# Pinning GpSimd's and TensorE's order in a loop over 64 experts, and taking GpSimd's weight splits to VectorE

## The chip, the cores and the metric

The kernel runs on one core of one Trainium2 chip. The metric is device time in microseconds of one execution. In the profile PE is TensorE, DVE is VectorE, ACT is ScalarE, POOL is GpSimd and SP is SyncE, which here only issues DMAs.

## What is computed

One layer of a hybrid decoder for 520 tokens (512 of a prompt, 8 samples), d_model 1024: a state-space branch and a dilated-attention branch, a layer norm, then a mixture of 64 experts (each token goes to 8), a shared expert, a gated per-layer input and a second layer norm. The change lies in the mixture of experts alone:

```python
scores = jax.nn.sigmoid(jnp.einsum('nd,de->ne', xf, w['w_router']))
_, top_idx = lax.top_k(scores + w['router_bias'], TOP_K)
...
    xb = x_pad[tok]
    h = jax.nn.silu(xb @ w1[e]) * (xb @ w3[e])
    yb = (h @ w2[e]).astype(jnp.float32)
    return acc.at[tok].add(yb * g[:, None])
...
shared = (jax.nn.silu(xf @ w['ws1']) * (xf @ w['ws3'])) @ w['ws2']
```

## The kernel before, in words

Every f32 product is made of three fp32r products: a matrix is split into `hi` (its value rounded by ACT) and `lo` (the rest, a subtraction on another engine), and hi x hi, lo x hi and hi x lo are summed in PSUM (`split`, line 267).

The weights of an expert are six chunks of 128x1024 floats: four (`AT`) for the first product, 1024 to 512 columns, and two (`BT`) for the second, 256 to 1024. The class `Stream` (line 288) loads them through SP into 12 raw buffers (`raw2` and `pre`), and splits them into five pairs of buffers (tag `v`, `VB`). Chunks are listed in the order in which PE takes them: four of expert e, two of expert e-1. Line 333 gives the subtraction of one chunk in six to POOL, 63 in all; the rest are DVE's.

The experts are sorted by the number of their tokens, and `CAPS` holds the rows that each place may take, from 112 down to 56. The loop is at line 1599; round e has these pieces:

- `expert_in(e)` (line 1429): 24 matmuls of 512 columns with four chunks, then `ffn_mid`: a SiLU on ACT and a product on DVE (`hg`).
- `turn(e + 1)` (line 1418): eight transposes of the gathered rows `xg` of the next expert, and their split (`xgh` on ACT, `xgl` on DVE).
- `expert_out(e - 1)` (line 1437): 12 matmuls with two chunks, `y` (scaled by the gates) on ACT, and a scatter with addition by POOL into `accD` in DRAM (line 1451). There are two such sums; experts below `SECOND` = 50 alternate between them, later ones use the first.
- `ffn_turn(e)` (line 1258): the turning of the inner layer, two transposes of `hg` and their split (`hh`, `hl`).
- `fetch(e + 3)` (line 1408): `find` searches the rows of an expert by five small matmuls with a one-hot matrix (`oh`, of DVE) into the PSUM tile `x`, which DVE reduces (`both`) and makes into row numbers (`idx`); `gather` (line 1412) has POOL fetch those rows from DRAM into one of three buffers `xg`.
- From round 6 on a piece of side work in four of five rounds (lines 1621 to 1632): parts of the shared expert (`shared_more`, `shared_out`), the per-layer inputs (`layer_inputs`, 30 matmuls of 256 columns, 20 times), and at the end `second_sums` (line 1372), which loads the second DRAM sum through SP into a single buffer and adds it to the residual on POOL.

The side work and the search share the only buffer of the PSUM pool `psx` (line 1481). The tile framework puts every engine's instructions into an order by a planner that simulates the program. What `tc.keep_in_program_order` marks keeps the order of the program on its engine. For PE the flag `T.pinned` (line 207) does so; it is off in the loop.

Of the kernel before, what the change touches and what calls it, by code (L numbers as in the profile page):

```python
# [11 lines left out]
def _quiet(*args, **kwargs):  # L12
# [11 lines left out]
ALU = mybir.AluOpType  # L24
# [4 lines left out]
NT = 520  # L29
HALF = 260  # L30
TT = 104
NE = 64
FIXED = 2
CAPS = ([112] * 3 + [100] * 1 + [94] * 1 + [92] * 1 + [88] * 2 + [86] * 1 + [84] * 3 + [82] * 2 + [78] * 7 + [76] * 2 + [74] * 4
        + [72] * 5 + [70] * 4 + [68] * 4 + [66] * 5 + [64] * 7 + [62] * 3 + [60] * 2 + [58] * 2 + [56] * 5)
# [16 lines left out]
SECOND = 50  # L52
# [148 lines left out]
def trunk_step(ctx: ExitStack, tc: tile.TileContext, I, O):  # L201
    nc = tc.nc
    V, S, G = nc.vector, nc.scalar, nc.gpsimd
# [15 lines left out]
    T = Tensor()  # L219
# [41 lines left out]
    def add(e, o, a, b):  # L261
        return e.tensor_tensor(out=o, in0=a, in1=b, op=ALU.add)
# [4 lines left out]
    def split(hi, lo, src, e=V):  # L267

        a = S.activation(hi, src, AF.Copy)  # L269
        return a, sub(e, lo, src, hi.bitcast(F32))  # L270
# [17 lines left out]
    class Stream:  # L288
# [34 lines left out]
        def split_to(self, n):  # L323
            while self.done < min(n, len(self.srcs)):
                p, tag, bufs = self.pools(self.done, 1)
                if p is None:
                    return
                self.load_to(self.done + 1)
                raw, was = self.raw.pop(self.done)
                hi = p.tile([128, 1024], F32R, tag=tag + "h", bufs=bufs, name="hi")  # L330
                lo = p.tile([128, 1024], F32R, tag=tag + "l", bufs=bufs, name="lo")
                m = self.done - P2 - 2
                split(hi, lo, raw, G if 0 < m < 6 * (NE - 1) and m % 6 == 2 else V)
                self.parts[self.done] = (hi, lo)
                self.done += 1
                self.held[was] -= 1
                self.load_to(self.done + 40)
# [7 lines left out]
    P2 = 48  # L345
    AT, BT = {}, {}

    H, EX = {}, {}
# [67 lines left out]
    xD = dram.tile([NT, 1024], F32, name="xD")  # L416
    sumsD = [dram.tile([640, 1024], F32, name=f"accD{n}") for n in range(2)]
# [840 lines left out]
    def ffn_turn(hg, m):  # L1258
        ps = bank()
        for k in range(2):  # L1260
            T.transpose(ps[:, m * k:m * k + m], hg[0:m, 128 * k:128 * k + 128], ident[0:m, 0:m])
        hh, hl = (moe.tile([128, 2, MAX_CAP], F32R, tag=nm, bufs=2, name=nm)[:, :, 0:m] for nm in ("hh", "hl"))
        H['turned'] = split(hh, hl, ps[:, 0:2 * m].rearrange("p (k t) -> p k t", k=2))
        return hh, hl
# [94 lines left out]
    def last_scales(i):  # L1359

        if i < 0:
            H['ln2'] = pw.tile([TT, 2, 1024], F32, tag="ph", name="ln2")
            H['rows'] = pw.tile([1, 2, 1024], F32, tag="pl", name="rows")
            nc.sync.dma_start(H['rows'], I['rows'][None, 2:4])
        else:
            for h in range(2):
                c = slice(512 * h, 512 * h + 512)
                ps = psx.tile([128, 512], F32, tag="x", name="x")[0:TT]
                T.matmul(ps, lhsT=H['ones'], rhs=H['rows'][:, i, c], start=True, stop=True)
                S.activation(H['ln2'][:, i, c], ps, AF.Copy)  # L1370

    def second_sums(i):

        t = pw.tile([128, 1024], F32, tag="praw", name="second")[0:TT]
        nc.sync.dma_start(t, sumsD[1][TT * i:TT * i + TT])
        add(G, H['x1'][:, i], H['x1'][:, i], t)


    XG, XT, HG, HT, GC, IX = {}, {}, {}, {}, {}, {}

    OH = {}

    def find(e, what=(0, 1)):

        m = CAPS[e]
        if e not in OH:
            OH[e] = one_hot(e, m)
# [19 lines left out]

    def fetch(e):
        find(e)
        gather(e)  # L1410

    def gather(e):
        m = CAPS[e]
        G.indirect_dma_start(out=XG[e % 3][0:m], out_offset=None, in_=xD[:, :],  # L1414
                             in_offset=bass.IndirectOffsetOnAxis(ap=IX[e][0:m, 0:1], axis=0),
                             bounds_check=NT - 1, oob_is_err=False)

    def turn(e):
        x, m = XG[e % 3], CAPS[e]
# [17 lines left out]
    def expert_out(e):  # L1437
        ps, m = mm2(), CAPS[e]
        hh, hl = HT.pop(e)
        for k in range(2):  # L1440
            hi, lo = stream.get(BT[e] + k)
            for n, (l, w) in enumerate(((hh, hi), (hh, lo), (hl, hi))):
                for h in range(2):
                    T.matmul(ps[0:m, h], lhsT=l[:, k], rhs=w[:, 512 * h:512 * h + 512], start=(k == 0 and n == 0),
                             stop=(k == 1 and n == 2))
        if e >= NE - 2:
            kept(e, ps)
            return
        y = py.tile([MAX_CAP, 1024], F32, tag="y", bufs=YB, name="y")[0:m]
        S.activation(y.rearrange("p (h n) -> p h n", h=2), ps[0:m], AF.Copy, scale=GC.pop(e)[0:m])  # L1450
        G.indirect_dma_start(out=sumsD[e % 2 if e < SECOND else 0][:, :], out_offset=bass.IndirectOffsetOnAxis(ap=IX.pop(e)[0:m, 0:1], axis=0),  # L1451
                             in_=y, in_offset=None, compute_op=ALU.add)

    def kept(e, ps):

# [21 lines left out]
    def second_phase():  # L1477
# [9 lines left out]
        x1 = H['x1']  # L1487
# [108 lines left out]
        py = open_pool("py")  # L1596
        side = [(q, i) for q in range(-2, 4) for i in range(-1, 5)]
        side += [(4, -1), (4, 0), (4, 1)] + [(5, i) for i in R5]
        for e in range(NE + 1):
            if e == NE - 1:  # L1600
                last_rows()
            if 0 < e < NE:
                expert_in(e)
            if 0 < e < NE - 1:
                turn(e + 1)
            if e:
                expert_out(e - 1)
            else:
                H['shared'] = py.tile([128, 5, 2, 2, TT], F32R, tag="side", name="st")
                mids = py.tile([MAX_CAP, 1024], F32, tag="y", bufs=YB, name="mids")  # L1610
                mids = [shared_mid(H['first half'][i], mids[0:TT, 128 * i:128 * i + 128]) for i in R5]
            if 0 < e < 6:
                shared_turn(mids[e - 1], e - 1, 0)
            if 0 < e < NE - 1:
                HT[e] = ffn_turn(HG.pop(e), CAPS[e])
            if e + 3 < NE:
                fetch(e + 3)
            if e == 4:
                close_pool(pre)
                pw = open_pool("pw")  # L1620
            while side and (e - 4) * SIDE >= N_SIDE - len(side) + 1:
                q, i = side.pop(0)
                if q == -2:
                    shared_more(i)
                elif q == -1:
                    shared_out(i)
                elif q < 4:
                    layer_inputs(q, i)
                elif q == 5:
                    second_sums(i)  # L1630
                else:
                    last_scales(i)
        assert not side
        acc = {}
        for i in R5:
# [216 lines left out]
```

## Time and profile before

| what | us |
|---|---|
| median of 3 runs | 1363.4 |
| lowest and highest of them | 1359.24, 1363.55 |
| the profiled execution | 1371.03 |
| its span, from the first to the last instruction | 1369.2 |
| busy in the span: PE, DVE, ACT, POOL | 1191.9, 970.3, 700.3, 560.2 |
| PE's mean granted clock | 0.928 of full |

The profile is of one execution; a busy time is the time in which an engine had an instruction under way, and the busy times of engines overlap. A matmul's row is longer than the distance to the next one, since matmuls are pipelined, so that PE's pace is read from the starts. A wait names what ended last before an instruction started. The granted clock is 1 at 2.4 GHz and 0.5 at 1.2 GHz. The DMA share is the mean busy share of the 16 DMA engines.

### The profile page before, as it was taken

What the parts mean: (1) busy time and instruction counts of PE and PEld (TensorE: products, weight loads), DVE (VectorE), ACT (ScalarE), POOL (GpSimd) and SP (SyncE); (2) the same over time, 40 slices, a digit from 0 to 9 for tenths busy, and PEclk for the clock granted to TensorE, in tenths of its full rate; (3) what the DMA queues carried; (4) which work ended last, traced back from release to release, by engine and by line L of the source; (5) the groups of instructions that cost most, each with busy time, mean ns of one, the idle gap of its engine ahead of it and who ended that gap; (6) DMA issues with size and microseconds to landing.
All of it is one profiled execution on the core that took longest, in us unless ns stands there. A gap on an engine that the chain in (4) does not pass through costs nothing. (4 is left out here: it accounts for less than half of the span.)

```text
span 1369.2 us, 20382 instructions
## 1 busy us (share of the span) xinstructions
PE 1191.9 (87%) x7082; PEld 890.2 (65%) x7084; DVE 970.3 (71%) x1397; ACT 700.3 (51%) x1055; POOL 560.2 (41%) x327
## 2 busy tenths in 40 slices
PE   7699899999997979787899688899999998968783
PEld 7699799999877756565566466576666664434441
DVE  7873748633588877576788578789789777647656
ACT  4131534222213766566567456767567665546562
POOL 1821231010124436243565354465664644464326
PEclk9898899999997989898999899999999999788896
DMA  7476553442512989798899798999999899887773
GB/s 286 134 240 120 191 182 105 118 116 92 191 60 89 294 222 314 226 286 262 257 319 319 224 274 275 310 306 305 303 300 321 288 301 266 224 229 243 260 191 100
DMA packets 114182, 312.93 MB, mean 229 GB/s; under 512 B 36986, under 2 KB 37410, under 8 KB 113000
## 3 DMA queue, kind: packets, MB, share of 16 engines
q1 hardware_dynamic: 68892, 249.24, 54.2%
q0 software_dynamic: 30208, 41.20, 14.0%
q10 hardware_dynamic: 14974, 21.14, 5.9%
q8 instruction: 57, 0.93, 0.3%
q14 instruction: 51, 0.42, 0.1%
HBM read 276.32 MB, written 32.87 MB: 226 GB/s over the span
## 5 line engine op out<-in xcount | busy, mean ns | idle before, releaser
L265 DVE TENSOR_TENSOR lo<-raw,hi 128x1024 fp32r<-128x1024 f32 x371 | 552.6, 1503 | 170.1 <-ACT hi L269 166.0
L269 ACT ACTIVATE hi<-raw 128x1024 fp32r<-128x1024 f32 x434 | 450.9, 1056 | 253.4 <-DMA raw<-in_we_dram 80.0
L1451 POOL DMA_INDIRECT accD<-y,idx x62 | 137.0, 2210 | 267.2 <-ACT hh L269 118.2
L210 PE MATMUL a<-hi,xgh 128*64 128x512 f32 (+18 forms) x512 | 211.8, 414 | 8.8 <-DVE xgl L265 6.0
L210 PE MATMUL a<-lo,xgh 128*64 128x512 f32 (+18 forms) x512 | 210.1, 410 | 7.3 <-DVE lo L265 7.3
L210 PE MATMUL a<-hi,xgl 128*64 128x512 f32 (+18 forms) x512 | 206.9, 404 | 0.0
L265 POOL TENSOR_TENSOR lo<-raw,hi 128x1024 fp32r<-128x1024 f32 x63 | 169.3, 2687 | 46.6 <-ACT hi L269 34.8
L1414 POOL DMA_INDIRECT xg<-xD,idx x64 | 125.0, 1953 | 146.5 <-DVE idx L1396 105.1
L210 PE MATMUL mm<-xh,hi 128*128 128x260 f32 (+1 forms) x576 | 121.7, 293 | 19.1 <-DVE r L259 10.7
L210 PE MATMUL mm<-xl,hi 128*128 128x260 f32 (+1 forms) x576 | 120.2, 291 | 0.8 <-DVE xl L265 0.8
L210 PE MATMUL mm<-xh,lo 128*128 128x260 f32 (+1 forms) x576 | 120.5, 291 | 0.0
L210 PEld LDWEIGHTS a<-hi,xgh 128*64 128x64 f32 (+18 forms) x512 | 75.7, 148 | 53.3 <-DVE xgl L265 7.6
L210 PEld LDWEIGHTS a<-lo,xgh 128*64 128x64 f32 (+18 forms) x512 | 75.6, 148 | 48.4 <-DVE lo L265 11.6
L210 PEld LDWEIGHTS mm<-xh,hi 128*128 128x128 f32 x576 | 92.8, 197 | 20.1 <-issue 11.0
L210 PE MATMUL mm<-lo,hh 128*64 128x512 f32 (+18 forms) x256 | 88.3, 428 | 18.3 <-POOL lo L265 17.8
L210 PEld LDWEIGHTS a<-hi,xgl 128*64 128x64 f32 (+18 forms) x512 | 75.5, 147 | 41.1 <-issue 4.0
L215 PE MATMUL a<-ident,xg 64*128 64x64 f32 (+18 forms) x512 | 57.7, 243 | 46.8 <-DMA xg<-xD,idx 38.5
L215 PEld LDWEIGHTS a<-ident,xg 64*128 64x128 f32 (+18 forms) x512 | 49.6, 148 | 73.0 <-DMA xg<-xD,idx 26.4
L210 PE MATMUL mm<-hi,hh 128*64 128x512 f32 (+18 forms) x256 | 88.0, 425 | 8.8 <-ACT hh L269 8.8
L1450 ACT ACTIVATE y<-mm,both 78x1024 f32<-78x1024 f32 (+19 forms) x62 | 68.8, 1109 | 52.1 <-PE mm L210 35.4
L210 PEld LDWEIGHTS mm<-xl,hi 128*128 128x128 f32 x576 | 92.2, 195 | 1.3 <-DVE xl L265 1.1
L210 PEld LDWEIGHTS mm<-xh,lo 128*128 128x128 f32 x576 | 92.4, 195 | 0.1
(410 smaller groups left out, 1999.1 us busy)
## 6 DMA issues: line engine op xcount, KB each, us to landing
raw<-in_we_dram SPq DMA_DIRECT2D x384, 512.0 KB
raw<-in_wd_dram SPq DMA_DIRECT2D x50, 512.0 KB
accD<-zeros_b POOLq DMA_DIRECT2D x2, 2560.0 KB
praw<-in_wp_dram SPq DMA_DIRECT2D x8, 512.0 KB
base<-in_xtok_dram ACTq DMA_DIRECT2D x1, 2080.0 KB
xD<-base ACTq DMA_DIRECT2D x5, 416.0 KB
second<-accD SPq DMA_DIRECT2D x5, 416.0 KB
acc<-accD SPq DMA_DIRECT2D x5, 416.0 KB
```

The lines of the kernel that those rows point to most:

```text
L210: ins = nc.tensor.matmul(*a, **k)
L215: ins = nc.tensor.transpose(*a, **k)
L265: return e.tensor_tensor(out=o, in0=a, in1=b, op=ALU.subtract)
L269: a = S.activation(hi, src, AF.Copy)
L1414: G.indirect_dma_start(out=XG[e % 3][0:m], out_offset=None, in_=xD[:, :], in_offset=bass.IndirectOffsetOnAxis(ap=IX[e][0:m, 0:1], axis=0), ...
L1450: S.activation(y.rearrange("p (h n) -> p h n", h=2), ps[0:m], AF.Copy, scale=GC.pop(e)[0:m])
L1451: G.indirect_dma_start(out=sumsD[e % 2 if e < SECOND else 0][:, :], out_offset=bass.IndirectOffsetOnAxis(ap=IX.pop(e)[0:m, 0:1], axis=0), ...
```

## The change

`split` of weight chunks is always ACT's and DVE's. `second_sums` adds on DVE. The expert's scatter is cut out of `expert_out` into a function of its own, `scatter`; gathers and scatters are kept in program order, which is now the gather of e+4, then the scatter of e-1 (round 0 fetches 3 and 4). `T.pinned` is on in the loop, and in PE's program order `ffn_turn(e)` stands at the end of the round, behind the side work.

```diff
--- before.py
+++ after.py
@@ -329,8 +329,7 @@
                 raw, was = self.raw.pop(self.done)
                 hi = p.tile([128, 1024], F32R, tag=tag + "h", bufs=bufs, name="hi")
                 lo = p.tile([128, 1024], F32R, tag=tag + "l", bufs=bufs, name="lo")
-                m = self.done - P2 - 2
-                split(hi, lo, raw, G if 0 < m < 6 * (NE - 1) and m % 6 == 2 else V)
+                split(hi, lo, raw)
                 self.parts[self.done] = (hi, lo)
                 self.done += 1
                 self.held[was] -= 1
@@ -1373,12 +1372,12 @@
 
         t = pw.tile([128, 1024], F32, tag="praw", name="second")[0:TT]
         nc.sync.dma_start(t, sumsD[1][TT * i:TT * i + TT])
-        add(G, H['x1'][:, i], H['x1'][:, i], t)
+        add(V, H['x1'][:, i], H['x1'][:, i], t)
 
 
     XG, XT, HG, HT, GC, IX = {}, {}, {}, {}, {}, {}
 
-    OH = {}
+    OH, YE = {}, {}
 
     def find(e, what=(0, 1)):
 
@@ -1407,13 +1406,13 @@
 
     def fetch(e):
         find(e)
-        gather(e)
+        tc.keep_in_program_order(gather(e))
 
     def gather(e):
         m = CAPS[e]
-        G.indirect_dma_start(out=XG[e % 3][0:m], out_offset=None, in_=xD[:, :],
-                             in_offset=bass.IndirectOffsetOnAxis(ap=IX[e][0:m, 0:1], axis=0),
-                             bounds_check=NT - 1, oob_is_err=False)
+        return G.indirect_dma_start(out=XG[e % 3][0:m], out_offset=None, in_=xD[:, :],
+                                    in_offset=bass.IndirectOffsetOnAxis(ap=IX[e][0:m, 0:1], axis=0),
+                                    bounds_check=NT - 1, oob_is_err=False)
 
     def turn(e):
         x, m = XG[e % 3], CAPS[e]
@@ -1448,8 +1447,14 @@
             return
         y = py.tile([MAX_CAP, 1024], F32, tag="y", bufs=YB, name="y")[0:m]
         S.activation(y.rearrange("p (h n) -> p h n", h=2), ps[0:m], AF.Copy, scale=GC.pop(e)[0:m])
-        G.indirect_dma_start(out=sumsD[e % 2 if e < SECOND else 0][:, :], out_offset=bass.IndirectOffsetOnAxis(ap=IX.pop(e)[0:m, 0:1], axis=0),
-                             in_=y, in_offset=None, compute_op=ALU.add)
+        YE[e] = y
+
+    def scatter(e):
+        y, m = YE.pop(e), CAPS[e]
+        sums = sumsD[e % 2 if e < SECOND else 0]
+        tc.keep_in_program_order(G.indirect_dma_start(
+            out=sums[:, :], out_offset=bass.IndirectOffsetOnAxis(ap=IX.pop(e)[0:m, 0:1], axis=0),
+            in_=y, in_offset=None, compute_op=ALU.add))
 
     def kept(e, ps):
 
@@ -1596,6 +1601,7 @@
         py = open_pool("py")
         side = [(q, i) for q in range(-2, 4) for i in range(-1, 5)]
         side += [(4, -1), (4, 0), (4, 1)] + [(5, i) for i in R5]
+        T.pinned = True
         for e in range(NE + 1):
             if e == NE - 1:
                 last_rows()
@@ -1605,16 +1611,17 @@
                 turn(e + 1)
             if e:
                 expert_out(e - 1)
-            else:
+            for n in (3, 4) if e == 0 else (e + 4,):
+                if n < NE:
+                    fetch(n)
+            if e - 1 in YE:
+                scatter(e - 1)
+            if e == 0:
                 H['shared'] = py.tile([128, 5, 2, 2, TT], F32R, tag="side", name="st")
                 mids = py.tile([MAX_CAP, 1024], F32, tag="y", bufs=YB, name="mids")
                 mids = [shared_mid(H['first half'][i], mids[0:TT, 128 * i:128 * i + 128]) for i in R5]
             if 0 < e < 6:
                 shared_turn(mids[e - 1], e - 1, 0)
-            if 0 < e < NE - 1:
-                HT[e] = ffn_turn(HG.pop(e), CAPS[e])
-            if e + 3 < NE:
-                fetch(e + 3)
             if e == 4:
                 close_pool(pre)
                 pw = open_pool("pw")
@@ -1630,6 +1637,9 @@
                     second_sums(i)
                 else:
                     last_scales(i)
+            if 0 < e < NE - 1:
+                HT[e] = ffn_turn(HG.pop(e), CAPS[e])
+        T.pinned = False
         assert not side
         acc = {}
         for i in R5:
```

How the planned orders of three engines changed, where it matters below. POOL before, at the experts with 74 rows (`xg` rows are gathers, `accD` rows scatters, `lo` rows the splits):

```order
L1451 DMA accD_148<-y,idx 640x1024
L265 TENSOR_TENSOR lo<-raw,hi 128x1024
L1414 DMA xg_4189<-xD,idx 74x1024
L1414 DMA xg_4185<-xD,idx 74x1024
L1414 DMA xg_4187<-xD,idx 74x1024
L1451 DMA accD_147<-y,idx 640x1024
L265 TENSOR_TENSOR lo<-raw,hi 128x1024
L1451 DMA accD_148<-y,idx 640x1024
```

POOL now, at the same experts:

```order
L1413 DMA xg_4189<-xD,idx 74x1024
L1455 DMA accD_147<-y,idx 640x1024
L1413 DMA xg_4185<-xD,idx 74x1024
L1455 DMA accD_148<-y,idx 640x1024
L1413 DMA xg_4187<-xD,idx 74x1024
L1455 DMA accD_147<-y,idx 640x1024
L1413 DMA xg_4189<-xD,idx 74x1024
L1455 DMA accD_148<-y,idx 640x1024
```

Three gathers stood in a row behind a split, and the scatters between splits; now gather and scatter take turns, with no split between them.

PE before, around one search for 68 rows (`what` is the search's last matmul, `mm` the second product, `pTs` the first matmuls of side work):

```order
L210 LDWEIGHTS oh
L210 MATMUL x<-what,oh 68x6
L210 MATMUL mm<-lo,hh 70x512 x2
L210 MATMUL mm<-hi,hl 70x512 x2
L210 MATMUL mm<-hi,hh 70x512 x2
L210 MATMUL mm<-lo,hh 70x512 x2
L210 MATMUL mm<-hi,hl 70x512 x2
L210 MATMUL x<-ph,pTs 104x256
L210 MATMUL x<-pl,pTs 104x256
```

PE now, around a search for 68 rows:

```order
L210 LDWEIGHTS oh
L210 MATMUL x<-what,oh 68x6
L210 LDWEIGHTS oh
L210 MATMUL x<-what,oh 68x6
L210 MATMUL x<-ph,pTs 104x256
L210 MATMUL x<-pl,pTs 104x256
L210 MATMUL x<-ph,pTs 104x256 x2
L210 MATMUL x<-pl,pTs 104x256
```

Most of the second product stood between search and side work; now the side work follows the search at once.

DVE now, in the rounds of experts 52 and 53 (`second` rows are the second sums, which were POOL's):

```order
L262 TENSOR_TENSOR base<-base,second 104x1024
L1395 TENSOR_SCALAR idx<-both,slots 60x1
L265 TENSOR_TENSOR hl<-a,hh 128x2x62
L265 TENSOR_TENSOR lo<-raw,hi 128x1024
L262 TENSOR_TENSOR base<-base,second 104x1024
L265 TENSOR_TENSOR lo<-raw,hi 128x1024 x2
L259 TENSOR_TENSOR hg<-hg,a 62x256
L265 TENSOR_TENSOR lo<-raw,hi 128x1024
L265 TENSOR_TENSOR xgl<-a,xgh 128x4x62 x2
L262 TENSOR_TENSOR base<-base,second 104x1024
```

Three of the five second sums stand among the splits of two rounds.

## Rows read from the trace of the kernel before

**Rows 1.** Windows: stretch, length, busy PE PEld DVE ACT POOL, clock, DMA share, GB/s.

```profile
470.00:614.00 144.00, 119.22 (x623) 85.04 (x622) 103.83 (x138) 87.58 (x124) 64.03 (x31) 0.92 0.89 265
614.00:749.00 135.00, 116.62 (x610) 77.84 (x611) 106.18 (x141) 87.70 (x118) 67.14 (x30) 0.94 0.91 287
749.00:893.00 144.00, 119.92 (x677) 82.57 (x675) 106.41 (x131) 87.83 (x123) 64.48 (x29) 0.94 0.90 274
893.00:1023.00 130.00, 121.66 (x741) 85.95 (x740) 109.86 (x144) 86.94 (x121) 77.84 (x32) 0.99 0.94 302
1023.00:1148.00 125.00, 121.69 (x704) 79.79 (x702) 102.75 (x136) 86.65 (x121) 60.81 (x30) 1.00 0.92 298
1148.00:1321.00 173.00, 135.68 (x569) 69.34 (x567) 106.89 (x124) 89.34 (x126) 81.88 (x39) 0.83 0.82 240
470.00:1321.00 851.00, 734.79 (x3914) 480.53 (x3913) 635.92 (x808) 526.07 (x728) 416.18 (x189) 0.93 0.89 275
```

**Rows 2.** Windows of 50 us in the loop: the highest DMA share.

```profile
700.00:750.00 50.00, 47.79 (x260) 31.83 (x259) 44.11 (x62) 36.10 (x48) 29.59 (x13) 1.00 0.99 322
```

**Rows 3.** Waits of PE in the loop: releaser, us in total, times, longest.

```profile
PE a L215 <- DMA xg<-xD,idx: 38.1, 8, 9.7
PE mm L210 <- POOL lo L265: 17.8, 11, 7.2
PE a L215 <- DVE hg L259: 17.1, 11, 3.4
PE x L210 <- DVE both L1393: 3.6, 3, 1.9
```

**Rows 4.** Waits of POOL in the loop, same columns.

```profile
POOL xg L1414 <- DVE idx L1396: 92.4, 20, 11.1
POOL accD L1451 <- ACT y L1450: 72.4, 12, 9.8
```

**Rows 5.** The page's groups of DVE's and POOL's splits; then min/median/max of DVE's.

```profile
L265 DVE TENSOR_TENSOR lo<-raw,hi 128x1024 fp32r<-128x1024 f32 x371 | 552.6, 1503 | 170.1 <-ACT hi L269 166.0
L265 POOL TENSOR_TENSOR lo<-raw,hi 128x1024 fp32r<-128x1024 f32 x63 | 169.3, 2687 | 46.6 <-ACT hi L269 34.8
...
L265 DVE TENSOR_TENSOR lo<-raw,hi x371: 1200/1216/6842, 5.9 to 1329.6; 128x1024 fp32r<-128x1024 f32 x186
```

**Rows 6.** Timeline: splits by DVE that meet one by POOL, and one that doesn't.

```profile
902.17 4.93 DVE L265 TENSOR_TENSOR lo<-raw,hi 128x1024 fp32r<-128x1024 f32 x2
902.48 2.39 POOL L265 TENSOR_TENSOR lo<-raw,hi 128x1024 fp32r<-128x1024 f32 x1
...
907.97 1.21 DVE L265 TENSOR_TENSOR lo<-raw,hi 128x1024 fp32r<-128x1024 f32 x1
```

**Rows 7.** Timeline of one round: start, length, engine, line, operation.

```profile
903.62 0.31 PE L210 MATMUL x<-what,oh 104*70 104x6 bf16 x5
...
906.38 0.66 PE L215 MATMUL a<-ident,xg 70*128 70x70 f32 x8
...
907.02 0.41 DVE L259 TENSOR_TENSOR hg<-hg,a 70x256 f32<-70x256 f32 x1
...
907.41 1.06 ACT L269 ACTIVATE hi<-raw 128x1024 fp32r<-128x1024 f32 x1
...
909.10 0.80 DVE L265 TENSOR_TENSOR xgl<-a,xgh 128x280 fp32r<-128x280 f32 x2
...
911.50 0.40 PE L210 MATMUL a<-hi,xgh 128*70 128x512 f32 x1
...
915.66 0.39 PE L210 MATMUL a<-hi,xgh 128*70 128x512 f32 x1
```

**Rows 8.** Timeline: SP issues the first second sum, POOL adds it.

```profile
1146.11 0.39 SPq L1375 DMA_DIRECT2D second<-accD  x1
...
1161.12 2.40 POOL L262 TENSOR_TENSOR base<-base,second 104x1024 f32<-104x1024 f32 x1 [3.75 <-DMA second<-accD]
```

## The prediction, on record before the change was run

> **What bounds the kernel now.** I read the busy time by stage first, because the shares of the whole span mix five stages with different limits. The loop over experts runs from 470 to 1321 us, 851 us of the 1369.2 us span. Cut at every tenth expert's output, its six stretches [rows 1] show two resources near their ends. The DMA engines are busy 0.89 to 0.94 of the first five, and 0.82 of the last. The best 50 us of the loop had 0.99 [rows 2]. PE is busy 121.7 of 125 us in the fifth stretch and 135.7 of 173 in the last, where it also ran at a granted clock of 0.83. No stretch is held by DVE alone: it is busy 635.9 of 851 us, 75%.
>
> Second, the list of waits says who stops PE [rows 3]: gathered rows that are late (38.1 us), a split by POOL that is late (17.8), the inner layer not yet formed (17.1), and only 3.6 us for the reduction behind the search. So the loop is a DMA-fed pipeline in which PE is stopped now and then, mostly by things that POOL does late. While PE stands, the raw buffers fill and the DMA engines run out of work as well.
>
> Third, why POOL is late: its own waits [rows 4]. In its queue a gather for a later expert stands behind a scatter that waits for an output, and the other way round.
>
> Fourth, the two kinds of split [rows 5]. DVE's median is 1216 ns, its mean 1503 ns over 371. The reason shows in three rows [rows 6]: two DVE splits that meet a split by POOL take 4.93 us together, and one that meets none takes 1.21.
>
> **The change, part by part.** *The 63 splits that go from POOL to DVE.* DVE gets 63 x 1.216 = 76.6 us. It loses what the meetings cost, at most (1.503 - 1.216) x 371 = 106.5 us [rows 5]. Net it has 30 us less to do, if every long split was long for that reason, and 77 more if none was. [Rows 6] is on the first side, so I take -30 for its load. DVE bounds no stretch, so by itself this is worth nothing in time. It takes away PE's wait for POOL's splits.
>
> The rule for such meetings is in the Trainium skill, SBUF — State Buffer, section Who interferes with whom: DVE with two SBUF inputs and a GpSimd instruction that reads SBUF exclude each other for a whole instruction. By it DVE could lose up to 63 x 2.687 = 169 us to POOL's splits; the trace's mean bounds it at 106.5, and my sum of time has neither.
>
> *The order of POOL.* In each round it is now gather for e+4, then scatter of e-1. The gather is asked for one round earlier than before and no longer comes in bunches, so I let the 38.1 us of [rows 3] go. Bound: none of it if gathers land later, all of it if they land in the two rounds that they have.
>
> *The order of PE.* Per round: first product, turning of the next expert's rows, second product, search, side work, and the turning of the inner layer at the end. The inner layer has then had the second product's time to form, so the 17.1 us go too. What is late next is the search: its bank is the single buffer that the side work uses, and PE may start the side work only when DVE has reduced the search. Before, the scheduler put other matmuls between. PE's own time from the first product's end to the search's end is 8 transposes (0.66), 12 matmuls at (915.66 - 911.50)/18 = 0.23 (2.8) and the search (0.31): 3.8 us [rows 7]. In that time DVE has hg, two splits and two xgl ahead of the reduction: 0.4 + 2.4 + 0.8 = 3.6 [rows 6, 7]. But the second of those splits needs a buffer that the first half of the second product frees (0.66 + 1.4), then ACT's 1.06 and DVE's 1.21, so the reduction comes at about 5 us. The wait per round with side work is thus 1.2 us, one split; its bounds are 0 and 3.6 (all of that DVE work still ahead when the search ends).
>
> *The second sums.* Five adds of 1024 columns go from POOL (2.40 us [rows 8]) to DVE, some 1.2 us by the split of the same length. In the new order of DVE three of them stand within ten rows, before splits whose raw data come earlier in SP's queue than the sums do. A first sum took from its issue at 1146.11 to the add at 1161.12 to be there [rows 8]. DVE may now stand, with the splits behind it. Bounds: 0 (the DMA queue has work meanwhile) and 5 x 15 = 75 us. I take 8 us, twice the one wait that POOL shows there (3.75), since DVE comes to it sooner.
>
> **The sum**, by stretch [rows 1]. Each stretch ends at the larger of two floors. The DMA floor is its DMA share times its length, divided by 0.97, a little under the best [rows 2]. The PE floor is PE's busy time at full clock (busy minus (1 - clock) x length, since a stretch at half speed doubles the work in it) plus 1.2 us for each side piece (3, 7, 7, 7 and 6 of them in the first five stretches, by the loop's own schedule of side work).
> - 470 to 614: DMA 0.89 x 144 / 0.97 = 132.1; PE 119.2 - 11.5 + 3.6 = 111.3. So 132.1.
> - 614 to 749: 126.6; PE 108.5 + 8.4 = 116.9. So 126.6.
> - 749 to 893: 133.6; PE 111.3 + 8.4 = 119.7. So 133.6.
> - 893 to 1023: 126.0; PE 120.4 + 8.4 = 128.8. So 128.8.
> - 1023 to 1148: 118.6; PE 121.7 + 7.2 = 128.9. So 128.9, 4 us longer than now.
> - 1148 to 1321: 146.2; PE 106.3. With the 8 us of the second sums, 154.2.
>
> Together 804.2 against 851, 46.8 us less. Before 470 and after 1321 us I cost the change at nothing: only the numbering of a few instructions moves there. The profiled execution took 1371.0 us, so 1324 in its terms. It is 7.6 us above the median of the runs shown, 1363.4, so I give **1316.6 us**.
>
> **The rivals.** *Fed as before.* If DMA reaches only 0.92 in a stretch, because shares of 0.94 and more were seen mainly where PE was busiest, the six come to 139.3, 133.6, 140.9, 132.8, 128.9 and 154.2: 829.7, a gain of 21 us, 1342. For it: PE's waits may move to raw data. Against: 0.99 in [rows 2].
>
> *Everything clears.* DMA at 0.99, no wait for the reduction, no loss at the second sums: 129.5, 124.1, 130.9, 123.4, 121.7, 146.0, together 775.6 and 75 us less: 1288.
>
> *PE stands behind the search* (slower). Same place as my 1.2 us, but DVE runs behind. The sum reaches 851 when the wait is 3.8 us, about the upper bound of 3.6. At 4.9 (one split more) the PE floors are 122, 143, 146, 155 and 151, the sum with 132.1 and 154.2 is 880, 29 us more: 1393. For it: DVE takes instructions strictly in its order, and the single bank. Against: before, this wait was 3.6 us in all. A standing DVE at the second sums, up to 75 us, would come on top.
>
> *DVE is saturated.* If the long splits were not POOL's doing, DVE gets 77 + 6 us more and, if it paced the loop, the time would be 1363.4 + 83 = 1446. 25% of idle time speaks against. The Trainium skill, Perfetto Trace Analysis, section Optimizing Scalar/DVE Operations, says that offloading from a saturated DVE, even to GPSIMD, may make sense, with a shared port that may spoil it; undoing the offload would cost by the first half and pay by the second. By that rule the trace decides, and [rows 6] agrees with the second half.
>
> *Nothing.* The tables of order show that the pins take hold on PE and POOL, so an unchanged time would need gains and new waits to cancel.
>
> **How the numbers follow.** Forecast within 1296 to 1332: 0.50. Fed as before: 0.17. Everything clears: 0.11. Behind the search: 0.13, DVE saturated: 0.02, cancelled: 0.07. A measurement here can tell about 0.3%, 4 us. Faster 0.77 (the first three, less a little), same 0.08, slower 0.15. The range runs from 1284, just past the case that all clears, to 1367, past the cancelled case, and leaves out the slower ones.
>
> **What would show it.** Right: no DVE split much over 1.22 us; the wait for gathered rows and for POOL gone from PE's list; DMA share 0.95 or more in the first five stretches; granted clock near 1 from 614 to 1148 and higher after. Right on the new wait: PE waiting for the reduction at the side work, some 1 us, about 30 times. Wrong: a long wait of DVE for the second sums with the DMA share falling, rounds of 14 us and more with side work, or PE waiting for DVE's splits throughout.

## The result and the profile after

The change made the kernel slower: 1433.45 us median (1425.05 to 1436.12, 4 runs) against 1361.32 us (4 runs of the kernel before), ratio 1.0519, 95% interval 1.0469 to 1.0569. The profiled execution spans 1423.3 us, 54 us more than before. It is the shortest of its four, and the profiled one before (1371.03 us) lies above its median, so the profiles show 54 of the 72 us between the medians. All 54 lie in the loop over experts, which takes 905 us (469 to 1374) instead of 851.

The windows of the loop after, cut at the same outputs as [rows 1], with the same columns:

```profile
469.00:626.00 157.00, 112.70 (x596) 80.69 (x594) 96.81 (x144) 86.88 (x123) 36.50 (x20) 0.88 0.82 246
626.00:783.00 157.00, 124.11 (x622) 83.41 (x622) 104.87 (x149) 90.27 (x122) 32.40 (x20) 0.90 0.82 247
783.00:934.00 151.00, 121.98 (x683) 87.25 (x684) 98.87 (x148) 87.02 (x119) 35.02 (x20) 0.91 0.84 260
934.00:1069.00 135.00, 120.66 (x721) 85.62 (x720) 98.43 (x148) 87.72 (x121) 32.53 (x20) 0.97 0.91 284
1069.00:1202.00 133.00, 124.47 (x721) 82.61 (x720) 99.05 (x149) 88.03 (x121) 34.30 (x20) 0.99 0.91 282
1202.00:1374.00 172.00, 131.87 (x566) 69.12 (x565) 98.84 (x139) 89.05 (x125) 36.95 (x22) 0.83 0.78 243
469.00:1374.00 905.00, 735.79 (x3905) 488.71 (x3904) 596.86 (x871) 528.96 (x726) 207.71 (x122) 0.91 0.84 259
```

PE's busy time is what it was (735.8, before 734.8) and DVE's is 39 us less. The DMA share fell to 0.84, and share times length is unchanged: 0.84 x 905 = 760, before 0.89 x 851 = 757. Nearly the same busy time moved the same bytes (259 GB/s x 905 us, before 275 x 851), so the transfers as a whole did not get slower; the DMA engines stood without work for some 50 us more. The first three stretches lost 42 us together and the next two 13.

PE's waits in the loop after (releaser, us in total, times, longest):

```profile
PE x L210 <- DVE both L1392: 70.2, 32, 11.8
PE a L215 <- DVE hl L265: 17.2, 5, 6.6
PE a L215 <- DVE sg L259: 15.0, 5, 12.3
PE a L215 <- DVE st L265: 13.8, 2, 12.7
PE a L215 <- DVE hg L259: 12.8, 6, 5.6
```

The late gathers and POOL's splits of [rows 3] are gone. The search, 3.6 us before, now holds PE for 70.2 us. ACT's list (waits for a scatter's landing and for raw weights) changed as much; before:

```profile
ACT hi L269 <- DMA raw<-in_we_dram: 79.6, 50, 3.8
ACT y L1450 <- DMA accD<-y,idx: 16.4, 4, 8.4
```

and after:

```profile
ACT y L1449 <- DMA accD<-y,idx: 80.9, 10, 15.5
ACT hi L269 <- DMA raw<-in_we_dram: 43.3, 25, 5.0
```

The first line is new in size. The output `y` is written by ACT into one of two buffers, and ACT must wait until the scatter that reads the buffer has landed in DRAM. How one such wait runs through the kernel is seen at 474 to 500 us, in pieces of the timelines of POOL, ACT, DVE and PE (in this order; in brackets the idle time before and its releaser):

```profile
473.97 1.65 POOL L1455 DMA_INDIRECT accD<-y,idx  x1 [0.31 <-issue]
...
493.94 1.11 ACT L1449 ACTIVATE y<-mm,both 112x1024 f32<-112x1024 f32 x1 [15.46 <-DMA accD<-y,idx]
494.95 1.05 ACT L269 ACTIVATE hi<-raw 128x1024 fp32r<-128x1024 f32 x1
495.90 0.25 ACT L269 ACTIVATE st<-a 128x104 fp32r<-128x104 f32 x1
...
496.03 1.22 DVE L265 TENSOR_TENSOR lo<-raw,hi 128x1024 fp32r<-128x1024 f32 x1 [15.32 <-ACT hi L269]
497.17 0.26 DVE L265 TENSOR_TENSOR st<-a,st 128x104 fp32r<-128x104 f32 x1
...
497.48 1.51 PE L215 MATMUL a<-ident,xg 94*128 94x94 f32 x8 [12.67 <-DVE st L265]
```

The scatter issued at 473.97 is waited for until 493.94. In ACT's order the next weight roundings stand behind `y`, and they start at once after it, without a wait for their raw data; DVE waits for them, PE for DVE, and the raw buffers stay full: SP issues no load of expert weights between 476 and 500 us. In the window from 488 to 497 us almost nothing is loaded (DMA share 0.08) and PE is not busy:

```profile
488.00:497.00 9.00, 0.00 (x0) 0.00 (x0) 0.97 (x1) 3.06 (x5) 1.52 (x1) 0.56 0.08 23
```

In rounds 1 to 5 one of the two `y` buffers even belongs to `mids` (in the kernel before too), so that each output waits for the last one's scatter.

The longest wait at the search, at 709 us, shows the other chain, in the timelines of DVE and of PE:

```profile
703.91 1.23 DVE L265 TENSOR_TENSOR lo<-raw,hi 128x1024 fp32r<-128x1024 f32 x1 [2.54 <-ACT hi L269]
705.06 0.87 DVE L265 TENSOR_TENSOR xgl<-a,xgh 128x312 fp32r<-128x312 f32 x2
708.07 1.23 DVE L265 TENSOR_TENSOR lo<-raw,hi 128x1024 fp32r<-128x1024 f32 x1 [2.15 <-ACT hi L269]
709.21 0.15 DVE L1392 TENSOR_REDUCE both<-x 78x2 f32<-78x6 f32 x1
...
709.42 0.76 PE L210 MATMUL x<-ph,st 128*104 128x512 f32 x1 [11.82 <-DVE both L1392]
```

The reduction needs 0.15 us and its input had long been there: PE's 11.82 us of idling begin where the search ends. The reduction stands in DVE's queue behind splits that wait for ACT, which waits for weights still under way (ACT's rows are in the last section). PE stands with it.

The two waits lie in different stretches. Of the 70.2 us at the search 25.5 are in the second stretch and 19.1 in the third, which are 22 and 7 us longer than before. Of the 80.9 us at `y` 40.9 are in the first stretch, 13 us longer, and 34.1 in the last, which is no longer than before: there they stand in the place of other waits. Nor does a scatter land later as a rule. From its issue to its landing (min/median/max in us), before and after:

```profile
DMA to landing us min/median/max: 6.6/11.8/21.4
DMA to landing us min/median/max: 4.5/10.9/33.1
```

### The profile page after: what moved, and what is told of

The parts are those of the page before. It is cut to its first block, busy times and chain, and to the rows that moved or that the text cites. A ratio compares the mean times of both kernels' runs of the same rounds, so it can differ in the third digit from the quotient of the medians.

```text
span 1423.3 us, 20324 instructions
## 1 busy us (share of the span) xinstructions
PE 1193.7 (84%) x7083; PEld 897.5 (63%) x7084; DVE 932.1 (65%) x1465; ACT 704.4 (49%) x1055; POOL 350.7 (25%) x259
## 5 line engine op out<-in xcount | busy, mean ns | idle before, releaser
L265 DVE TENSOR_TENSOR lo<-raw,hi 128x1024 fp32r<-128x1024 f32 x434 | 534.7, 1241 | 241.8 <-ACT hi L269 236.8
L1413 POOL DMA_INDIRECT xg<-xD,idx x64 | 101.5, 1586 | 616.3 <-issue 364.2
L210 PE MATMUL a<-hi,xgh 128*64 128x512 f32 (+18 forms) x512 | 213.7, 417 | 20.3 <-ACT hi L269 12.7
L1455 POOL DMA_INDIRECT accD<-y,idx x62 | 113.8, 1835 | 120.2 <-DMA accD<-y,idx 51.9
L1449 ACT ACTIVATE y<-mm,both 78x1024 f32<-78x1024 f32 (+19 forms) x62 | 68.8, 1110 | 94.6 <-DMA accD<-y,idx 80.9
L210 PEld LDWEIGHTS mm<-xh,hi 128*128 128x128 f32 x576 | 91.4, 194 | 22.1 <-issue 12.8
L210 PE MATMUL mm<-lo,hh 128*64 128x512 f32 (+18 forms) x256 | 83.3, 408 | 7.0 <-DVE lo L265 7.0
L210 PE MATMUL mm<-hi,hl 128*64 128x512 f32 (+18 forms) x256 | 82.4, 404 | 0.0
L215 PE MATMUL a<-ident,xg 64*128 64x64 f32 (+18 forms) x512 | 48.7, 236 | 31.1 <-DVE hl L265 17.2
L215 PEld LDWEIGHTS a<-ident,xg 64*128 64x128 f32 (+18 forms) x512 | 43.7, 143 | 48.8 <-DVE hl L265 18.0
```

Of the source, the lines that this page charges most:

```text
L210: ins = nc.tensor.matmul(*a, **k)
L215: ins = nc.tensor.transpose(*a, **k)
L265: return e.tensor_tensor(out=o, in0=a, in1=b, op=ALU.subtract)
L1413: return G.indirect_dma_start(out=XG[e % 3][0:m], out_offset=None, in_=xD[:, :], in_offset=bass.IndirectOffsetOnAxis(ap=IX[e][0:m, 0:1], a ...
L1455: tc.keep_in_program_order(G.indirect_dma_start(out=sums[:, :], out_offset=bass.IndirectOffsetOnAxis(ap=IX.pop(e)[0:m, 0:1], axis=0), in_= ...
```

## The experiments

Two theories. *S*: PE is held by the search, whose reduction stands behind DVE's splits. *D*: ACT is held at `y` by the scatter's landing. Rivals: that the fixed order of PE is a cost as such, that DVE has too much to do now, or that the gather takes the scatter's place in the queue. In the expectations of the first runs A is S, B is that DVE has too much to do, and C is that the cost lies in POOL's order, of which D is the precise form. Waits named below are of each run's own loop.

**1. The search early.** `find(e + 4)` goes right behind the first product; the gather stays.

```diff
                 expert_in(e)
+            for n in soon:
+                find(n)
             if 0 < e < NE - 1:
                 turn(e + 1)
...
-                    fetch(n)
+                tc.keep_in_program_order(gather(n))
```

> The changed kernel with one move: the search for expert e+4 stands right behind the first product in PE's round instead of right before the side work; its gather stays where it was. Theory A (PE stands before the side work, because the reduction of the search is behind splits on DVE that wait for raw weights): the waits of PE for the reduction, 70 us in all in the changed kernel, fall under 10 us, and the time to 1345 to 1370 us. Theory B (DVE has too much with all 63 splits): no more than 15 us better, 1418 to 1433. Theory C (a scatter that stands behind a gather in POOL's queue is late, so that the output's buffer is late on ACT): the gather still waits in the same place, so 1415 to 1433.

Measured: 1394.88 us, ratio 1.0215 (1.0157 to 1.0274). The search's waits fell from 70.2 to 13.5 us and the time by 38.6 us, less than theory A gave. S holds for that part, but half of the loss stays, with ACT's 59.4 us at `y`:

```profile
PE x L210 <- DVE both L1392: 13.5, 5, 7.2
ACT y L1449 <- DMA accD<-y,idx: 59.4, 8, 13.5
```

**2. PE free.** In the changed kernel the line `T.pinned = True` is taken out.

> The changed kernel with PE's order in the loop left to the planner again; POOL's pinned order and the splits by ACT and DVE stay. Theory A: the side work moves away from the search, the waits for the reduction fall to some 10 us, 1330 to 1370 us. Theory B: DVE's load is unchanged, so 1415 to 1435. Theory C: POOL's order is unchanged, so 1410 to 1435.

Measured: 1415.37 us, 1.0367 (1.0309 to 1.0425). The search's waits fell to 13.6 us, as A said, but not the time: ACT's waits at `y` rose to 134.4. The time is in the ranges of B and C; experiment 3 tells these two apart. The scheduler didn't repair POOL's order from PE's side, which speaks for D.

**3. POOL's splits back.** In the changed kernel, `split(hi, lo, raw)` with POOL for one chunk in six again.

> The changed kernel with one chunk in six split by POOL again; PE's and POOL's pinned orders stay. Theory B: back to 1360 to 1375 us. Theory A: PE still stands at the side work, and now also behind POOL's splits, 1430 to 1470 us, with DVE's mean split near 1.5 us again. Theory C: the scatters are later still, 1430 to 1460.

Measured: 1438.84 us, 1.0554 (1.0504 to 1.0605): the changed kernel's time. Search 71.9 us, POOL's splits 32.5 in PE's list. The moved splits neither cost nor gave anything clear there; B falls, and DVE's load isn't the cause. That the scatters are later still, as C had it, didn't come: ACT's waits at `y` are 56.5 us, not 80.9.

**4. The splits alone.** The kernel before with the `split` line of the change and nothing else.

> The kernel before with one edit: all chunks are split by ACT and DVE. Nothing is pinned that was not. Theory A: the lock between POOL and DVE goes, PE no longer waits for POOL's splits (18 us before), 1335 to 1360 us. Theory B: DVE paces the loop, 1400 to 1440. Theory C says nothing of it: 1340 to 1365.

Measured: 1407.91 us, 1.0358 (1.0295 to 1.042). The time is above the ranges of A and C and in the range that "DVE has too much to do" gave, but for another reason: DVE's busy time in the loop went down (593 us, before 636). PE's list shows why:

```profile
PE a L215 <- DMA xg<-xD,idx: 90.6, 15, 15.5
```

Without the splits in POOL's queue the planner put POOL's gathers elsewhere, behind scatters, and they came late.

**5. POOL's order alone.** The kernel before with `scatter` cut out and gather and scatter kept in program order; PE free, splits and second sums as before.

```diff
+            for n in (3, 4) if e == 0 else (e + 4,):
+                if n < NE:
+                    fetch(n)
+            if e - 1 in YE:
+                scatter(e - 1)
...
-            if e + 3 < NE:
-                fetch(e + 3)
```

> The kernel before with POOL's gathers and scatters pinned in the order of the change (gather of e+4, then scatter of e-1); POOL keeps its splits and second sums, PE is free. Theory A (only PE's standing at the search costs): gathers come earlier, nothing stands at the search, 1345 to 1370 us. Theory D (the scatter's rows follow the gather's in one DMA queue and land late, so that ACT stands at the output y with its two buffers, and every later rounding behind it): ACT's waits of y for the landing, 16 us in the kernel before and 81 in the changed one, are 60 us or more, and the time is 1385 to 1420.

Measured: 1403.28 us, 1.0259 (1.0171 to 1.0348). PE's wait for gathers fell from 38.1 to 15.3 us, as the prediction wanted, and this came instead:

```profile
ACT y L1450 <- DMA accD<-y,idx: 109.0, 15, 19.5
```

**6. The scatter first.** Experiment 1 with `scatter(e - 1)` ahead of the gather.

> The run with the early search, and in POOL's pinned order the scatter of e-1 before the gather of e+4. Theory D: the waits of y fall from 59 to under 30 us, 1365 to 1385 us. Rival: the landing is slow because of the weights' traffic, not the gather's place: y waits the same, 1390 to 1400 us; and if gathers are now late, PE waits for gathered rows and it is over 1400.

Measured: 1390.76 us, 1.020 (1.0135 to 1.0265), ACT's wait at `y` 51.8 us, not under 30: a gather ahead of it isn't what makes the scatter late. What does stays open.

**7. Three outputs.** Experiment 1 with `YB = 3`, for which SBUF must give up a raw buffer, `RAW2 = 6`.

> The run with the early search, with three buffers of y for two, paid for by six raw buffers for seven. Theory D: ACT's waits of y nearly vanish (under 10 us), and the time falls to 1365 to 1390 although one chunk less is loaded ahead. Rival (what limits is how far the weights are loaded ahead): slower than the early search, 1400 to 1425.

Measured: 1382.71 us, 1.0141 (1.0069 to 1.0213). The waits at `y` are gone; those for raw data rose from 87.1 to 125.7:

```profile
ACT hi L269 <- DMA raw<-in_we_dram: 125.7, 78, 5.7
ACT y L1449 <- DMA accD<-y,idx: 1.0, 1, 1.0
```

D holds: the loop became shorter in the first and the last stretch, where the waits at `y` were (158 to 144 and 167 to 156 us). Part of what this gives is paid back.

**8. The shared expert's turning later.** Experiment 1 with `shared_turn` of `shared_more` moved behind the next round's first product, so that PE no longer waits for `sg`.

> The run with the early search, and the turning of the shared expert's inner layer, for which PE stood 19.5 us behind its own side piece in five rounds, moved behind the first product of the next round. If what PE stands for is lost: 1375 to 1385 us. If those waits lie beside others (y's, the weights'): 1388 to 1398.

Measured: 1401.46 us, 1.027 (1.0207 to 1.0333). That is above both ranges. The wait for `sg` fell from 19.5 to 1.3 us and nothing was gained; that for `hg` rose from 30.6 to 44.6.

**9. Scatter first and three outputs**, 6 and 7 together.

> The run with the early search, three y buffers and six raw buffers (1382.7 us), with the scatter ahead of the gather as well. Theory D (ACT stands at y until a scatter has landed; the third buffer has taken those waits away): the scatter's place has nothing left to give, 1375 to 1388 us. Rival (the scatter's landing itself, late in the round, collides with the weights' loads): it starts earlier, waits of ACT for raw data fall, and the time is 1365 us or less. Neither reaches the kernel before if the remaining 20 us are the lost raw buffer's.

Measured: 1387.39 us, 1.0156 (1.0103 to 1.0208): the scatter's place has nothing left to give.

**10. PE's order alone.** The kernel before with `T.pinned` on in the loop and `ffn_turn` last; `fetch(e + 3)`, splits and POOL's freedom as before.

> The kernel before with PE's order alone: the flag T.pinned on in the loop, the turning of the inner layer last in the round; splits, second sums, the search's place (e+3) and the scheduler's freedom on POOL as before. Theory S (PE standing at side work behind the search's reduction costs some 38 us whatever POOL does): PE's waits at side work for DVE come to 50 us or more, 1385 to 1415 us. Rival P (the costs come with POOL's pinned order and with the moved splits, and PE's order alone is harmless or a gain, as the prediction had it): PE's waits for the search are about 1 us a round, 30 us or less in all, and the time is 1340 to 1366 us.

Measured: 1454.21 us, 1.0637 (1.0574 to 1.0701), the slowest of all. The rival (harmless) falls. S is right in direction, but the search's waits stay under the 50 us that it wanted and the time is above its range, so the loss isn't theirs alone:

```profile
PE a L215 <- DMA xg<-xD,idx: 75.3, 11, 16.3
PE x L210 <- DVE both L1393: 43.4, 32, 4.2
```

With PE fixed, the planner lets scatter and gather e+3 take turns on POOL, each gather behind a scatter that waits for its output. In the change, with the gather for e+4 ahead of the scatter, PE's list has no wait for gathers.

**11. Three outputs in the kernel before**, `YB = 3` and `RAW2 = 6`.

> The kernel before with three y buffers and six raw buffers, nothing else. In the kernel before ACT waits 16.4 us for a scatter's landing, so the third buffer can give at most that. Theory R (one raw buffer fewer costs what the run with three y buffers shows, some 20 us of its distance to the kernel before): 1366 to 1385 us. Rival (six raw buffers feed as well as seven, and the remaining distance comes from the pinned orders): 1345 to 1363 us.

Measured: 1412.81 us, 1.0359 (1.0308 to 1.041), above both expectations. ACT's wait for raw data is 119.0 us (79.6), and PE's for gathers 49.8 (38.1), probably since the planner's order moved again. How the loss divides between the two stays open.

**12. Two gather buffers, three outputs, seven raw buffers.** Experiment 7, with each gather two rounds ahead and first in POOL's round, so that two `xg` buffers do, and the seventh raw buffer back.

```diff
-RAW2 = 6
+RAW2 = 7
...
-        x, m = XG[e % 3], CAPS[e]
+        x, m = XG[e % 2], CAPS[e]
...
+            if e + 2 < NE:
+                tc.keep_in_program_order(gather(e + 2))
             soon = ...
```

> The run with the early search, three y buffers and six raw buffers (1382.7 us), with the gathers issued first in POOL's round and only two rounds ahead, so that two xg buffers are enough; the 4 KB this gives go back to the raw buffers, seven again. Theory R (the 20 us by which that run still lost to the kernel before are the lost raw buffer: ACT waited 125.7 us for raw data there, 79.6 in the kernel before): raw waits fall under 100 us and the time is 1345 to 1370 us. Rival G (a gather that has only one round to land is late, as in the runs in which the scheduler placed gathers behind scatters): PE waits 30 us or more for xg, 1380 to 1420 us. Rival O (the rest is PE's fixed order itself): no xg waits and still 1375 to 1390 us.

Measured: 1363.46 us, ratio 0.9985 (0.9954 to 1.0016): the kernel before, no faster. Its loop, 835 us long in the profiled execution, has a DMA share of 0.91, and ACT waits 83.0 us for raw data. R holds.

**13. The buffer given the other way**, `RAW2 = 8` and `YB = 2`.

> The same with the 4 KB given the other way: eight raw buffers and two y buffers. Theory D and R together say: ACT's waits for the scatter's landing come back (50 to 70 us in its list), and its waits for raw data fall to 70 us or less; an eighth buffer gives back part of what the scatter takes, 1370 to 1392 us (the early search with seven raw and two y buffers: 1394.9 us). Rival (the depth of loading alone decides, the scatter does not): below the run with three y buffers and seven raw buffers of this call.

Measured: 1372.9 us, 1.0022 (0.999 to 1.0055). ACT waits 40.5 us for raw data and 62.3 at `y`, both as expected:

```profile
ACT y L1450 <- DMA accD<-y,idx: 62.3, 11, 11.5
```

The two buffers are worth nearly the same. With as much waiting at `y` as experiment 1 this run is 22 us faster, so the gathers' place and the eighth raw buffer give something as well.

**14. PE free on that base**: experiment 12 without `T.pinned = True`.

> The run with two gather buffers, three y buffers and seven raw buffers (1363.5 us, as the kernel before), with PE left to the scheduler in the loop. Theory S (PE's fixed order costs by what it puts PE behind; with the search early little of that is left, some 17 us of waits at the search and 19 at the inner layer): free, the time moves by less than 1%, 1350 to 1375 us. Rival P (a fixed order on PE is a cost as such, the scheduler fills those waits): 1345 us or less. Rival Q (the scheduler's order on PE also decides when POOL gets rows and outputs, and gathers that have one round to land come late): 1380 us or more with PE waiting over 30 us for xg.

Measured: 1373.41 us, 1.0051 (1.0017 to 1.0085). Over the whole loop the fixed order on PE isn't a cost as such. PE's wait for gathers is 33.4 us against 16.9, past the bound that Q gave for that wait, but the time is within S's range.

**15. The search late on that base**: experiment 12 with `find` back behind the second product, as the change has it.

> The same run (1363.5 us) with the search back behind the second product, where the change has it, and all else kept. Theory S: on this better base, too, the search behind DVE's splits costs as much as the first experiment gained (38 us): PE's list shows 45 us or more for the reduction at side work, 1385 to 1410 us. Rival (the search's place cost much only while ACT stood at y behind it): the waits are 1.2 us a round as first worked out, 30 us or less in all, and the time is 1363 to 1378 us.

Measured: 1399.85 us, 1.0225 (1.0165 to 1.0284), 36 us above experiment 12, with

```profile
PE x L210 <- DVE both L1393: 64.5, 32, 7.0
```

With ACT no longer standing at `y`, the search costs about as much as in experiment 1. S is a cause of its own. Its size here isn't the search's alone: PE's waits for gathers rose too, from 16.9 to 31.5 us.

So two repairs give back the loss of 72 us: 38.6 us with the search early (36 on the other base), and 31 us more from experiment 1 to 12. How much of the 31 is the wait at `y` isn't isolated. Experiment 7 has 12 of them, with a raw buffer less; the other 19 came with the seventh raw buffer and the gathers' new place together. A run with that place, two outputs and seven raw buffers is missing.

The account holds for the sum of the stretches and not for each. The second stretch, 135 us before and 157 in the change, takes 150 us in experiment 12 and 138 with PE free (experiment 14):

```profile
608.00:758.00 150.00, 120.83 (x598) 78.37 (x598) 105.02 (x148) 90.07 (x121) 34.11 (x20) 0.91 0.87 264
617.00:755.00 138.00, 118.81 (x583) 78.94 (x584) 99.95 (x140) 87.02 (x118) 30.68 (x19) 0.91 0.89 279
```

So some 12 us there go with PE's fixed order on this base, beside S and D (one execution each; with PE free experiment 5, too, takes 155 us there). Experiment 12 makes up for them in the first, third and last stretch, which take 136, 133 and 159 us against 144, 144 and 173 before; experiment 14 loses them in the third (151 us), where PE waits 25.1 us for gathers. Which of PE's fixed places costs the 12 us was not tried.

## Why the prediction was wrong

**The splits: right, the gain smaller.** DVE's splits now take 1241 ns in the mean, 434 of them, against 1503 in [rows 5]; the page's row:

```profile
L265 DVE TENSOR_TENSOR lo<-raw,hi 128x1024 fp32r<-128x1024 f32 x434 | 534.7, 1241 | 241.8 <-ACT hi L269 236.8
```

The total is 534.7 us, 18 us less with 63 more of them; -30 was said. That its worth in time is nothing held as long as POOL's order stays fixed (experiment 3). The Trainium skill, SBUF — State Buffer, section Who interferes with whom, says that a DVE instruction with two SBUF inputs contends with a GpSimd instruction that reads SBUF. The trace agrees: without POOL's splits DVE's take 1241 ns in the mean, with them 1503. What wasn't seen: in the kernel before, the splits also shaped the planner's order of POOL, and taking them out alone costs 47 us (experiment 4).

**The order of POOL: right on what goes, wrong on what comes.** The 38.1 us of late gathers went. But the step looked only at the gather. "Gather for e+4, then scatter of e-1" also moves the scatter, and what is queued behind a waiting instruction wasn't asked of `y`: it waits for the scatter, and all weight roundings stand behind it on ACT. The wait was in the trace of before, 16.4 us in 4 waits, and the prediction gives it no price. It became 80.9 us, and 109.0 with POOL's order alone. This term was put at nothing; by experiments 7 and 12 it is worth between 12 and 31 of the 72 us.

**The order of PE: the place right, the size half right.** The new wait was named at the right place. Three pieces of PE's timeline:

```profile
814.47 0.36 PE L210 MATMUL x<-ph,pTs 128*104 128x256 f32 x1 [1.17 <-DVE both L1392]
...
963.75 0.37 PE L210 MATMUL x<-ph,pTs 128*104 128x256 f32 x1 [1.16 <-DVE both L1392]
...
798.02 0.54 PE L210 MATMUL x<-ph,pTs 128*104 128x256 f32 x1 [4.98 <-DVE both L1392]
```

24 of the 32 waits are at most 1.23 us, such as the first two, and for the reason that the step gave: the last thing ahead of the reduction is a split, here in DVE's timeline before PE's start at 814.47:

```profile
813.13 1.22 DVE L265 TENSOR_TENSOR lo<-raw,hi 128x1024 fp32r<-128x1024 f32 x1
814.26 0.15 DVE L1392 TENSOR_REDUCE both<-x 72x2 f32<-72x6 f32 x1
```

Eight waits are longer, like the third, up to 11.82 us; they hold 44.7 of the 70.2 us and make the mean 70.2 / 32 = 2.2. The bound of 3.6 us counted how long DVE's instructions take and not that a split ahead in the queue may itself wait for its weights. The inner layer's 17.1 us went only to 12.8.

**The second sums: about right.** DVE waited 12.7 us for them, where 8 was taken, and the last stretch is no longer than before (172 us, before 173):

```profile
DVE base L262 <- DMA second<-accD: 12.7, 4, 9.3
```

**The sum: the step that failed most.** It let each stretch end at the larger of a DMA floor and a PE floor. With the measured 2.2 us put into it, the PE floors of the first five stretches are 114, 124, 127, 136 and 135, and the sum is 132.1 + 126.6 + 133.6 + 136 + 135 + 154.2 = 817 us, still a gain of 34. The loop took 905. A maximum holds only while the DMA engines can run on when the consumers stand. They can't for long (DMA share 0.08 from 488 to 497 us, where ACT stood at `y`): my description counted 12 raw buffers, but the five of `pre` are given up in round 4, and from there loading is seven chunks, 1.2 experts, ahead. The sum let no wait through in its DMA-bound stretches. In experiment 15 against 12, PE's waits at the search grew by 47.8 us and the profiled execution by 48 (1359.64 to 1407.89; the medians by 36). In experiment 1 against the change they fell by 56.7 us and the profiled execution by 27 (1425.05 to 1398.3), while PE's waits for `hg` and `xgl` rose by 27. So between half and all of a wait came through. A share of 0.97, taken from the best 50 us [rows 2], was reached by no loop: the best, experiment 12, has 0.91. In the change the first five stretches have 0.82 to 0.91, where 0.95 or more was to show that the sum was right, and the clock from 626 to 1069 us is 0.90 to 0.97, where it was to be near 1.

**The rivals.** "PE stands behind the search" had the side and the place, with 1393 us; but its break-even of 3.8 us a round came from the same sum, while 2.2 already cost 36 to 39 us. "Fed as before" took 0.92, about what the best loop reached, but without a price for the waits. "DVE saturated" falls: DVE is busy 596.9 of 905 us, 66%. The scatter's part of the loss stood in no rival. Two sums of rivals were off, without changing their sides: in "Everything clears" the last stretch is 0.82 x 173 / 0.99 = 143.3, not 146.0, and "Fed as before" leaves out the 8 us of the second sums.

**The expected gain.** Where most of both new waits is taken away (experiment 12), the time is that of the kernel before, although half of the waits that the prediction let go is gone: late gathers 16.9 us (38.1 before), POOL's splits none (17.8), but the inner layer 19.9 (17.1). In the place of the rest PE waits for DVE at other points:

```profile
PE a L215 <- DVE hg L259: 19.9, 9, 7.7
PE a L210 <- DVE xgl L265: 18.9, 12, 5.5
PE a L215 <- DVE sg L259: 18.4, 5, 7.8
PE a L215 <- DMA xg<-xD,idx: 16.9, 5, 7.0
PE x L210 <- DVE both L1393: 16.7, 4, 7.2
```

In experiment 8 one of these waits was taken away and the next took its place. ACT's wait for raw weights stays, 83.0 us (79.6 before); that it stands behind all of them is likely and was not shown.

## What to carry to other kernels

When a step is moved in one in-order queue, follow its result as well as its input: who needs the buffer it frees, and what stands behind that instruction on its own engine. This loop, fed by transfers and seven chunks ahead, didn't end at the larger of two floors: between half and all of its consumers' waits were lost. In such a loop add the waits to the floor, count the buffers that are there in the stretch itself, and compare stretch by stretch, since a total can hide a loss in one behind a gain in another. Parts of a change of order don't add up: splits alone +47 us, POOL's order alone +40, PE's order alone +91, all three with the second sums +72.

## What the hardware showed unexpectedly

A scatter of at most 112 rows of 4 KB, with addition in DRAM, was waited for until 20 us after its issue (473.97 to 493.94, above), though the DMA share was only 0.08 from 488 to 497 us. The longest landing in the change took 33.1 us.

When ACT waits for weights, the DMA engines need not be busy. ACT's timeline and a window around 700 us:

```profile
698.74 1.06 ACT L269 ACTIVATE hi<-raw 128x1024 fp32r<-128x1024 f32 x1 [3.07 <-DMA raw<-in_we_dram]
...
702.83 1.06 ACT L269 ACTIVATE hi<-raw 128x1024 fp32r<-128x1024 f32 x1 [2.77 <-DMA raw<-in_we_dram]
...
706.98 1.06 ACT L269 ACTIVATE hi<-raw 128x1024 fp32r<-128x1024 f32 x1 [2.46 <-DMA raw<-in_we_dram]
...
700.00:710.00 10.00, 0.58 (x2) 0.45 (x3) 5.26 (x9) 2.81 (x5) 0.00 (x0) 0.54 0.52 168
```

Three loads of 512 KB were there one every 4.1 us, at a DMA share of 0.52 and 168 GB/s, where [rows 2] had 0.99 and 322. They weren't issued late: SP had issued eight loads between 682 and 698 us. Why these loads were slow while half of the DMA time was idle was not tried and stays open.
